# A hybrid decoder layer on one core: modulation sums, one feed-forward part and one x load put elsewhere

## The chip, the core and the metric

The kernel runs on one core of a Trainium2 chip. The core has a matrix engine (PE in the profile, with its weight loads as PEld), a vector engine (DVE), an activation engine (ACT), a general engine (POOL) and an engine that only issues transfers here (SP). Each engine works through its own instructions in order, and the engines wait for one another through semaphores. The metric is the time of one execution on the device in microseconds; lower is better. Shapes are partitions x elements.

## What is computed

One layer for a sequence of 1024 tokens of width 1024, in float32:

```python
mod = silu(cond) @ w_mod + b_mod            # nine vectors of 1024
sh1, sc1, g1, sh2, sc2, g2, sh3, sc3, g3 = split(mod, 9)

h = rms_norm(x) * (1 + sc1) + sh1
x = x + 0.5 * g1 * ((silu(h @ w_gate1) * (h @ w_up1)) @ w_down1)      # D_FF = 2816

h = rms_norm(x) * (1 + sc2) + sh2
b, c, v, u = split(h @ W_in, 4)                                       # 512 each
yA = b * causal_conv3(c * v)
yB = gelu(s5_scan(u) + D * u);  yB = yB * sigmoid(yB @ glu_w + glu_b)
x = x + g2 * (concat(rms_norm(yA), rms_norm(yB)) @ W_out)

h = rms_norm(x) * (1 + sc3) + sh3
x = x + 0.5 * g3 * ((silu(h @ w_gate2) * (h @ w_up2)) @ w_down2)
y = rms_norm(x)
```

## The kernel before

**Products.** Activations and weights are split into a high and a low half, and each product of a 128x128 weight with 128x512 activations is three matmuls (`mm3`, L333). The tokens are worked in two halves of 512 (h = 0, 1). The 2816 hidden columns of a feed-forward make 11 groups of 256.

**Seven products in place of eight.** In most groups the 2x2 block product of weights and activations is made by seven products of sums of blocks (`seven`, L575, gate first and then up). The sums of activations (A11, A12, A22, S1 to S4 in the code; tiles f, s and h3S in the profile) come from `combos` and `combos_last` (L543, L562) on DVE; the sums of weights (t1 to t4) are made on POOL by `combine` and `split_done` (L160, L168).

**Weights.** `stream` (L287) lists the weight arrays (1 MB each, tile raw) and the granules cut from them (tile w, two parts of 128x512, each with a high and a low half). `pump` (L182) makes the next granule when a ring slot is free: it loads the array if that isn't done, ACT copies the high half, and DVE subtracts to get the low half. Two raw tiles exist; a raw is reloaded when the granules before it have been cut. `take` hands granules to the products, `free` gives slots back.

**Which groups go where.** `LAST` (L39) names for each feed-forward the groups whose down projection is done plainly at its end. In the second feed-forward (names fb), group 0's four activation tiles stay in SBUF (`gu_evac`, L476) and its down projection (`down2`, L700: 96 matmuls and 16 DVE updates `x<-fb0d`) runs inside group 1, after the first of `seven`'s products. Groups 1 to 8 go to DRAM (`keep`, L482) and come back in `down7` (L655); groups 9 and 10 end it (the loop at the end of the kernel, tiles fb10d), where the last 256-token pieces of the final norm (n4, in the profile n_0 and n_256) follow.

**Modulation.** `mod_tile` (L466) makes a custom DVE instruction of 128x1024 (`wm<-wm,cact`, one eighth of a vector) and issues the fetch of a later array (512 KB, `wm<-in_wmod`). `side2` (L1132) makes them one at a time as a side task; `clock.period` says after how many clock ticks of the main work the next is put in. SC2, SH2 and G2 run from L1209 on, during the second half of the first feed-forward's down projection, into tiles of movA (a pool of 20). SC3, SH3 and G3 run from L1414 on, during the GLU and the output projection; for that the vector cact is written to DRAM at L849 and read back.

**The mixer.** `u` comes first (L1277 to L1292); as each of the four tiles ya0 to ya3 of u is done, `across` issues eight small transfers to u_d. The state space part goes in eight batches: `state_loads` (L1319) fetches ub, co and si; `states` (L1337) makes px on PE, copies it to X on ACT, swaps halves by transfers (swx), multiplies and scans on DVE, swaps again (swz) and adds to co on DVE; `outputs` (L1362) makes yy on PE, and then issues the fetches mk and mo for the next batch and ub, co, si for the one after that. The clock puts batch b's `states` and `outputs` among the matmuls of c and v (weights w103 to w110). cs is the tile in which c and v are multiplied. ub has two buffers; mi, mk and mo have one.

**Order.** The order on each engine is settled when the program is built, and differs from the order of the source lines. All transfers go through SP in order: one whose buffer is not free holds those behind it. They rotate over eight semaphores, so each waits for the one eight before it.

**x.** `load_x` (L327) brings x back in two parts after the side work; its second part (four transfers of 512 KB) is issued in `down7("fad0")` behind the product A12 of its first half (L1207).

Of the kernel before, what the change touches and what calls it, by code (L numbers as in the profile page):

```python
# [17 lines left out]
ALU = mybir.AluOpType  # L18
# [20 lines left out]
LAST = ((0, NGRP - 2, NGRP - 1), (NGRP - 2, NGRP - 1))  # L39
# [77 lines left out]
class Weights:  # L117
# [7 lines left out]

    def __init__(self, engines, srcs, granules, raw_bufs):
        self.V, self.A, self.SP, self.G = engines
        self.srcs, self.granules, self.raw_bufs = srcs, granules, raw_bufs
        self.left = [0] * len(srcs)
        self.combined = {j for pair in granules for j, c in pair if isinstance(c, str)}  # L130
        for pair in granules:
            for j, _ in pair:
                self.left[j] += 1
        self.raws, self.tiles, self.sums, self.kinds = [], [], {}, []
        self.given = self.freed = 0
        self.sums_pool = None
        self.slots = deque()
# [22 lines left out]
    def combine(self, j):  # L160

        f = self.sums_pool.tile([P, HALF], F32, tag="sums", name=f"sums{j}")[:]
        r = [self.raws[j][:, c * HALF : (c + 1) * HALF] for c in range(4)]
        self.G.tensor_tensor(out=f, in0=r[2], in1=r[1], op=ALU.subtract)  # L164
        self.G.tensor_tensor(out=r[1], in0=r[1], in1=r[0], op=ALU.subtract)  # L165
        self.sums[j] = {"t1": r[1], "t2": r[0], "t3": f, "t4": r[0]}

    def split_done(self, j, c):  # L168

        if j in self.combined and c in (0, "t2"):  # L170
            s, r = self.sums[j], self.raws[j][:, :HALF]
            if c == 0:
                self.G.tensor_tensor(out=r, in0=s["t3"], in1=r, op=ALU.add)  # L173
            else:
                self.G.tensor_tensor(out=r, in0=self.chunk(j, 3), in1=r, op=ALU.subtract)  # L175
# [56 lines left out]
def hymba_layer(ctx: ExitStack, tc, x_d, wm1_d, wmod_d, gu1_d, gs1_d, ds1_d, wl1_d, win_d, wout_d, glu_d, gu2_d, gs2_d, wd2_d, ds2_d, wl2_d, cols_d, cond_d, lam_d, bc_d, out_d):  # L232
# [54 lines left out]
    def stream(gu, gs, wd, ds, wl, m):  # L287


        for g in range(m):  # L290
            plain([gu[2 * g], gu[2 * g + 1]])
        for g in range(m, NGRP):
            j = len(srcs)
            inner = g == 1
            srcs.extend([gs[g - m, 0], wd, gs[g - m, 1]] if inner else [gs[g - m, 0], gs[g - m, 1]])
            seven = [(i, c) for i in (j, j + 1 + inner) for c in Weights.SEVEN]
            seven = [seven[i : i + 2] for i in range(0, 14, 2)]
            if inner:
                granules.extend(seven[:1] + [[(j + 1, 2 * q), (j + 1, 2 * q + 1)] for q in range(2)] + seven[1:])
            else:  # L300
                granules.extend(seven)
# [5 lines left out]
        plain([wl[i] for i in range(wl.shape[0])])  # L307

    stream(gu1_d, gs1_d, None, ds1_d, wl1_d, SEVEN_FROM[0])
    plain([win_d[i] for i in range(8)] + [glu_d] + [wout_d[i] for i in range(4)])  # L310
    stream(gu2_d, gs2_d, wd2_d, ds2_d, wl2_d, SEVEN_FROM[1])
    ws = Weights((V, A, SP, nc.gpsimd), srcs, granules, 2)
    ws.raw_pool = lambda i: rawp
# [162 lines left out]
    def gu_evac(fi, h, pg, pu, a_tiles, name):  # L476
        sg, af = t2k(f"{name}sg"), t2k(f"{name}af")
        A.activation(sg[:], pg[:], AF.Silu)
        V.tensor_tensor(out=af[:], in0=sg[:], in1=pu[:], op=ALU.mult)
        a_tiles[fi, h] = split_act(af[:], name + "a")  # L480

# [37 lines left out]

    def down(h, wd, groups, n, name, after):  # L520

        for d0 in range(0, KT, 4):
            outs = [ps(f"{name}d{d}_{h}") for d in range(d0, d0 + 4)]
            for q, a_tiles in enumerate(groups):
                for fi in range(2):
                    for i, o in enumerate(outs):
                        mm3(o[:], wd[2 * q + d0 // 4], 4 * fi + i, a_tiles[fi, h], q == fi == 0, q == len(groups) - 1 and fi == 1)
            for i, o in enumerate(outs):
                d = d0 + i
                V.scalar_tensor_tensor(out=x[d][h], in0=o[:], scalar=gate[:, n, d : d + 1], in1=x[d][h], op0=ALU.mult, op1=ALU.add)  # L530
                if after is not None:
                    after(d, h)
# [42 lines left out]
    def seven(name, between, place=1, kept=None, then=None):  # L575
# [4 lines left out]
        for side in "gu":  # L580
# [17 lines left out]
            for n, (left, b) in enumerate(SEVEN):  # L598
# [45 lines left out]
                if side == "g" and n == place:  # L644
                    between()
                if side == "u" and then is not None:
                    then(left)
        return a_tiles

# [50 lines left out]
    def down2(a_tiles, n, name, halves=(1, 0)):  # L700
        wd = ws.take(2)
        for dh in range(2):
            for h in halves:
                for i in range(4):
                    d = 4 * dh + i
                    o = ps(f"{name}d{d}_{h}")
                    for fi in range(2):
                        mm3(o[:], wd[dh], 4 * fi + i, a_tiles[fi, h], fi == 0, fi == 1)
                    V.scalar_tensor_tensor(out=x[d][h], in0=o[:], scalar=gate[:, n, d : d + 1], in1=x[d][h], op0=ALU.mult, op1=ALU.add)
            ws.free()  # L710

# [9 lines left out]
    es1 = ExitStack()  # L721
    cap = es1.enter_context(tc.tile_pool(name="cap", bufs=1))
# [126 lines left out]
    cact_d = scratch.tile([P, 1024], F32, name="cact_d")  # L849
    SP.dma_start(cact_d[:], cact[:])  # L850
# [345 lines left out]
    for g in range(SEVEN_FROM[0], NGRP):  # L1196
# [9 lines left out]
        seven(f"fa{g}", lambda: None, kept=kept[g], then=(lambda left: fetch_chunk(0, left)) if g == NGRP - 1 else None)  # L1206
# [71 lines left out]
    for h in range(2):  # L1278
# [8 lines left out]
        else:  # L1287
            ready(act2, h, KT)
            for i in range(4):
# [103 lines left out]

    wb = ws.take(4)
# [14 lines left out]
    mods_open = ExitStack()  # L1409
    wmp = mods_open.enter_context(tc.tile_pool(name="wmp2", bufs=1, side="right"))  # L1410
# [51 lines left out]
    clock.period = 1000  # L1462
# [11 lines left out]
    clock.period = 3  # L1474
# [8 lines left out]
    while clock.side:  # L1483
        clock.step()
    clock.period = 4
    mods_open.close()
    es2.close()
    movs["B"] = ctx.enter_context(tc.tile_pool(name="movB", bufs=12))
# [11 lines left out]
    ctx.callback(sums_open.close)  # L1500
    ctx.callback(first_open.close)

    def group0():

        a_tiles, pg, pu = {}, {}, {}
# [3 lines left out]
        gu_evac(0, 0, pg[0, 0], pu[0, 0], a_tiles, "fb0_0_0")  # L1509
# [5 lines left out]
        gu_evac(0, 1, pg[0, 1], pu[0, 1], a_tiles, "fb0_0_1")  # L1515
# [4 lines left out]
        for h in range(2):  # L1520
            gu_evac(1, h, pg[1, h], proj(u1, act3[h], f"fb0u1_{h}"), a_tiles, f"fb0_1_{h}")
        ws.free()
        return a_tiles

    clock.side.extend([combos(act3, "h3", "BAA"), combos_last(act3, "h3", "A")])
    a_prev = group0()
    kept = {g: kept_for(g, g not in LAST[1]) for g in range(1, NGRP - 1)}
    HOMES = dict(A11="B", S2="A", A12="B", S3="A", S1="B", A22="A", S4="A")
    lefts = [{left: [] for left in HOMES} for _ in range(CHUNKS)]
    a_last = {}  # L1530

    def fetch_last(left):
        if left == "A11":
            for h in range(2):
                for fi in range(2):
                    a_last[fi, h] = fetch(kept[NGRP - 2], f"A{h + 1}{fi + 1}", "B", f"fb{NGRP - 2}l")

    seven("fb1", lambda: down2(a_prev, 2, "fb0", (0, 1)), 0, kept[1])
    for g in range(2, NGRP - 1):
        seven(f"fb{g}", lambda: None, kept=kept[g])  # L1540
    a_prev = seven("fb10", lambda: None, then=lambda left: fetch_chunk(0, left, "fb"))
    down7("fbd0", lefts[0], 2, lambda left: fetch_chunk(1, left, "fb"))
    down7("fbd1", lefts[1], 2, fetch_last)
    n4 = {}
# [22 lines left out]

    for dh in range(2):
        wd = ws.take(2)
        for h in range(2):  # L1570
            for tok in PIECES[h] if dh else WHOLE:
                for i in range(4):
                    d = 4 * dh + i
                    o = ps(f"fb10d{d}_{h}_{tok.start}")
                    for q, (w, a) in enumerate(zip(wd, (a_last, a_prev))):
                        for fi in range(2):
                            mm3(o[:, tok], w, 4 * fi + i, a[fi, h], q == fi == 0, q == fi == 1, tok)
                    xs = x[d][h][:, tok]
                    V.scalar_tensor_tensor(out=xs, in0=o[:, tok], scalar=gate[:, 2, d : d + 1], in1=xs, op0=ALU.mult, op1=ALU.add)
                    for piece in PIECES[h] if not dh else [tok]:  # L1580
                        after2(d, h, piece)
        ws.free(2)
# [15 lines left out]
def _arrays(i):  # L1598
# [5 lines left out]
    for n in (1, 2):  # L1604
# [5 lines left out]
        if n == 2:  # L1610
            a["wd2"] = b[0].transpose(1, 2, 0, 3).reshape(P, 2, 1024)
# [31 lines left out]
_ORDER = ["x", "wm1", "wmod", "gu1", "gs1", "ds1", "wl1", "win", "wout", "glu", "gu2", "gs2", "wd2", "ds2", "wl2", "cols", "cond", "lam", "bc"]  # L1643
# [17 lines left out]
```

## Time and profile before

| | |
|---|---|
| runs, us | 1749.49 median of 3 (1746.47 to 1751.61) |
| profiled execution, its own time, us | 1752.1 |
| its span, first to last instruction, us | 1750.3 |
| mean granted PE clock | 0.989 |
| ACT, busy us (share) | 566.0 (32%) |
| POOL, busy us (share) | 351.1 (20%) |
| transfers, MB | 304.54 |
| share of the span on the chain that ended last | PE 76%, DVE 14%, DMA 5% |

The page gives each engine's busy time. A view of waits lists, for an engine, what it stood waiting for: us in total, how many times, and the longest. A view of windows gives each engine's busy time and instruction count in a stretch, with the TensorE clock granted in it, the share of time the transfer engines were busy and the rate in GB/s. In a timeline row stand the start, the duration, engine and line, the operation, output<-input, shape and how many instructions were joined; in brackets, the idle time before and what ended it. All instructions carry L107, the helper that records them, so tiles tell them apart.

### The profile page before, as it was taken

How to read it: one execution, taken by the hardware profiler on the slowest of the kernel's cores; microseconds unless marked ns; L12 is line 12 of the kernel's file. 1: busy time of each engine (PE TensorE's matmuls, PEld its weight loads, DVE VectorE, ACT ScalarE, POOL GpSimd, SP SyncE). 2: the span in 40 equal slices, each digit the busy share in tenths (PEclk: the TensorE clock that was granted, in tenths of full speed). 3: DMA queues.
4: the chain of work that ended last, by engine and by line, in shares of the span. 5: the costliest groups of instructions: out<-in, count | busy, mean ns of one | idle time of the engine just before them, and what ended most of it. 6: DMA issues, size and time to landing. Idle time of an engine off the chain costs nothing.

```text
span 1750.3 us, 20808 instructions
## 1 busy us (share of the span) xinstructions
PE 1677.9 (96%) x7532; PEld 1379.6 (79%) x7532; DVE 1300.6 (74%) x2286; ACT 566.0 (32%) x934; POOL 351.1 (20%) x241
## 2 busy tenths in 40 slices
PE   4999999999999999999999899989999999999996
PEld 3788887878787888887877778778888888888886
DVE  7999999999855687744656977967777666676656
ACT  4223234444322221332113424423343443322221
POOL 0000132222222221100000022023323322333211
PEclk9999999999999999999999999999999999999998
DMA  8245544444597877134654450113444334669312
GB/s 319 85 145 196 207 167 165 182 169 178 196 391 266 326 256 292 56 84 149 210 157 140 144 191 25 48 46 135 157 162 173 147 133 156 239 242 366 115 49 96
DMA packets 101080, 304.54 MB, mean 174 GB/s; under 512 B 19057, under 2 KB 34673, under 8 KB 89842
## 3 DMA queue, kind: packets, MB, share of 16 engines
q1 hardware_dynamic: 100978, 303.22, 48.4%
q8 instruction: 59, 0.97, 0.2%
q14 instruction: 43, 0.35, 0.1%
HBM read 212.47 MB, written 86.51 MB: 171 GB/s over the span
## 4 chain that ended last, share of the span: by engine, by line
PE 76%; DVE 14%; DMA 5%; issue 2%; POOL 1%; ACT 1%; SPq 1%; DVEq 0%; POOLq 0%; ACTq 0%
PE wo L107 4%; PE fald L107 3%; DVE w L107 3%; PE p L107 2%; PE fb10d L107 2%; PE fbd_0B L107 2%; PE fbd_1B L107 2%; PE u L107 2%; DMA swz<-si 2%; PE b L107 1%; DVE x L107 1%; PE c L107 1%; PE fa3u L107 1%; PE fb0g L107 1%; PE fa2g L107 1%
## 5 line engine op out<-in xcount | busy, mean ns | idle before, releaser
L107 ACT CAST w<-raw 128x512 fp32r<-128x512 f32 (+1 forms) x358 | 236.2, 689 | 484.3 <-issue 75.0
L107 DVE TENSOR_TENSOR w<-raw,w 128x512 fp32r<-128x512 f32 (+1 forms) x358 | 295.9, 845 | 107.3 <-ACT w L107 106.5
L164 POOL TENSOR_TENSOR sums<-raw 128x512 f32<-128x512 f32 x50 | 71.4, 1429 | 451.5 <-DMA raw<-in_gs 263.3
L173 POOL TENSOR_TENSOR raw<-sums,raw 128x512 f32<-128x512 f32 x50 | 77.7, 1554 | 371.1 <-DVE w L107 358.9
L175 POOL TENSOR_TENSOR raw<-raw 128x512 f32<-128x512 f32 x50 | 77.5, 1549 | 89.6 <-DVE w L107 73.0
L107 DVE CUSTOM_DVE_ANT_0 wm<-wm,cact 128x1024 f32<-128x1024 f32 x56 | 76.6, 1375 | 16.9 <-DMA wm<-in_wmod 16.9
L165 POOL TENSOR_TENSOR raw<-raw 128x512 f32<-128x512 f32 x50 | 77.3, 1547 | 3.2
L366 POOL TENSOR_TENSOR n3aq<-n3aq,n3aq 128x512 f32<-128x512 f32 x5 | 8.3, 1666 | 281.4 <-DMA wm<-in_wmod 255.7
L107 PE MATMUL p<-h,w 128*128 128x512 f32 x192 | 50.0, 423 | 8.0 <-DVE h L107 5.1
L107 DVE TENSOR_TENSOR w<-sums,w 128x512 fp32r<-128x512 f32 x50 | 52.5, 1063 | 3.6 <-ACT w L107 3.0
L107 PEld LDWEIGHTS p<-h,w 128*128 128x128 f32 x192 | 39.4, 207 | 18.4 <-DVE h L107 6.4
L107 PE MATMUL v<-h,w 128*128 128x512 f32 x192 | 46.9, 395 | 0.0
L107 PE MATMUL c<-h,w 128*128 128x512 f32 x192 | 46.6, 395 | 0.0
L107 PE MATMUL wo<-oa,w 128*128 128x512 f32 x192 | 45.6, 392 | 0.9 <-DVE w L107 0.7
L107 PE MATMUL b<-h,w 128*128 128x512 f32 x192 | 45.6, 394 | 0.0
L107 PE MATMUL wo<-ob,w 128*128 128x512 f32 x192 | 45.5, 392 | 0.0
L107 PE MATMUL u<-h,w 128*128 128x512 f32 x192 | 44.7, 392 | 0.2 <-DVE h L107 0.2
L107 PEld LDWEIGHTS wo<-oa,w 128*128 128x128 f32 x192 | 35.8, 188 | 9.0 <-DVE w L107 1.1
L107 PEld LDWEIGHTS u<-h,w 128*128 128x128 f32 x192 | 35.7, 188 | 8.2 <-DVE h L107 0.6
L107 PEld LDWEIGHTS wo<-ob,w 128*128 128x128 f32 x192 | 35.8, 188 | 7.7 <-DVE ob L107 0.4
L107 PEld LDWEIGHTS b<-h,w 128*128 128x128 f32 x192 | 35.6, 188 | 7.1
L107 PEld LDWEIGHTS c<-h,w 128*128 128x128 f32 x192 | 35.4, 188 | 7.0
(1565 smaller groups left out, 4056.2 us busy)
## 6 DMA issues: line engine op xcount, KB each, us to landing
raw<-in_gs SPq DMA_DIRECT2D x34, 1024.0 KB, 5.5
wm<-in_wmod SPq DMA_DIRECT2D x56, 512.0 KB, 5.3
raw<-in_ds SPq DMA_DIRECT2D x16, 1024.0 KB, 7.2
raw<-in_gu SPq DMA_DIRECT2D x10, 1024.0 KB, 7.0
mw<-in_wm SPq DMA_DIRECT2D x8, 1024.0 KB, 12.8
x<-in_x SPq DMA_DIRECT2D x16, 512.0 KB, 8.0
raw<-in_win SPq DMA_DIRECT2D x8, 1024.0 KB, 5.4
raw<-in_wl SPq DMA_DIRECT2D x5, 1024.0 KB, 6.7
```

Source lines behind the costliest of these rows:

```text
L107: r = getattr(self.engine, name)(*args, **kw)
L164: self.G.tensor_tensor(out=f, in0=r[2], in1=r[1], op=ALU.subtract)
L165: self.G.tensor_tensor(out=r[1], in0=r[1], in1=r[0], op=ALU.subtract)
L173: self.G.tensor_tensor(out=r, in0=s["t3"], in1=r, op=ALU.add)
L175: self.G.tensor_tensor(out=r, in0=self.chunk(j, 3), in1=r, op=ALU.subtract)
L366: nc.gpsimd.tensor_tensor(out=a, in0=a, in1=sq[:, :n], op=ALU.add)
```

## The change

It has four parts. Where the text below names A to D, it means these.

- **A.** Group 0 of the second feed-forward is kept in DRAM too, and its down projection is done with groups 9 and 10: three weights instead of two for each output, a third ring slot (ring1c), and for the first four outputs of the second half all four at a time.
- **B.** Group 1 of the second feed-forward has a function of its own (`seven_early`): A11, A12, A22 come before S1 to S4, and gate and up go side by side. Each granule takes one part from each of the two raw tiles, so that both raws are held until the group's last granule, w135.
- **C.** G2, SC3, SH3 and G3 (32 sums and 32 fetches) run in the second half of u and in the c and v stage, at period 3; cact stays in SBUF.
- **D.** The second part of the x load is issued behind the product A22 in place of A12.

```diff
-LAST = ((0, NGRP - 2, NGRP - 1), (NGRP - 2, NGRP - 1))
+LAST = ((0, NGRP - 2, NGRP - 1), (0, NGRP - 2, NGRP - 1))
...
+    EARLY = (0, 3, "t4", "t1", "t2", "t3", 2)
...
-        self.sums[j] = {"t1": r[1], "t2": r[0], "t3": f, "t4": r[0]}
+        self.sums[j] = {"t1": r[1], "t2": r[0], "t3": f, "t4": r[3 if j in self.early else 0]}
...
+        if j in self.early:
+            r0, r3 = (self.raws[j][:, q * HALF : (q + 1) * HALF] for q in (0, 3))
+            if c == 0:
+                self.G.tensor_tensor(out=r0, in0=self.sums[j]["t3"], in1=r0, op=ALU.add)
+            elif c == 3:
+                self.G.tensor_tensor(out=r3, in0=r3, in1=r0, op=ALU.subtract)
+            return
...
+            if g == 1:
+                two = j, j + 1
+                granules.extend([(j, c), (j + 1, c)] for c in Weights.EARLY)
...
+    EARLY = (("A11", "A"), ("A12", "A"), ("A22", "E"), ("S1", "C"), ("S2", "B"), ("S3", "D"), ("S4", "C"))
+
+    def seven_early(name, kept):
...
+        for left, b in EARLY:
+            (w,) = ws.take()
+            for q, side in enumerate("gu"):
+                bank, nm = banks[side], f"{name}{side}"
+                opens = b not in bank
+                if opens:
+                    bank[b] = ps(f"{nm}{b}")
+                for k in range(4):
+                    while len(blocks[left]) <= k:
+                        clock.step()
+                    mm3(bank[b][:], w, 4 * q + k, blocks[left][k], opens and k == 0, k == 3, more=not opens)
...
+                elif left == "S2":
+                    u2[side] = t2k(nm + "u2")
+                    add(u2, t1, side, "B")
+                elif left == "S3":
+                    u3[side] = t2k(nm + "u3")
+                    add(u3, u2, side, "D")
+                    add(t1, u3, side, "C")
...
+                elif left == "S4":
+                    add(u2, u2, side, "C")
...
+            ws.free()
...
-    cact_d = scratch.tile([P, 1024], F32, name="cact_d")
-    SP.dma_start(cact_d[:], cact[:])
...
-    down7("fad0", lefts[0], 0, lambda left: fetch_chunk(1, left), lambda left: load_x(range(2), (1, 3)) if left == "A12" else None)
+    down7("fad0", lefts[0], 0, lambda left: fetch_chunk(1, left), lambda left: load_x(range(2), (1, 3)) if left == "A22" else None)
     clock.period = 8
-    clock.side.append(side2(mod_mov, (SC2, SH2, G2)))
+    clock.side.append(side2(mod_mov, (SC2, SH2)))
...
             ready(act2, h, KT)
+            clock.period = 3
+            clock.side.append(side2(mod_mov, (G2, SC3, SH3, G3)))
...
+    while clock.side:
+        clock.step()
     wb = ws.take(4)
...
-    pools["cact"] = wmp.tile([P, 1024], F32, name="cact2")
-    SP.dma_start(pools["cact"][:], cact_d[:])
-    clock.period = 8
-    clock.side.append(side2(lambda name: wmp.tile([P, 1024], F32, tag="wm", name=name, bufs=2)[:], (SC3, SH3, G3)))
...
-        gu_evac(0, 0, pg[0, 0], pu[0, 0], a_tiles, "fb0_0_0")
+        gu_keep(0, 0, pg[0, 0], pu[0, 0], afs, kept, "fb0")
...
-    seven("fb1", lambda: down2(a_prev, 2, "fb0", (0, 1)), 0, kept[1])
+    seven_early("fb1", kept[1])
...
+    def last_part(dh, h, tok, tiles, free=False):
+        outs = {d: ps(f"fb10d{d}_{h}_{tok.start}") for d in tiles}
+        for q, (w, a) in enumerate(zip(wd, (*a_last, a_prev))):
+            for fi in range(2):
+                for d, o in outs.items():
+                    mm3(o[:, tok], w, 4 * fi + d % 4, a[fi, h], q == fi == 0, q == 2 and fi == 1, tok)
...
     for dh in range(2):
-        wd = ws.take(2)
+        wd = ws.take(3)
```

More of the change, by code (lines that the diff above doesn't have):

```diff
@@ L285, in plain, with stream @@
             srcs.append(a)
-    def stream(gu, gs, wd, ds, wl, m):
+    def stream(gu, gs, ds, wl, m):
+        two = ()
         for g in range(m):
@@ L518, in proj @@
         return o
[L520 to L532, printed above, removed]
     blocks = {}
@@ L573, in hymba_layer, with seven @@
     SECOND = (("A11", "A"), ("S2", "B"), ("A12", "A"), ("S3", "B"), ("S1", "C"), ("A22", "B"), ("S4", "C"))
-    def seven(name, between, place=1, kept=None, then=None):
+    def seven(name, kept=None, then=None):
         a_tiles, gate_, taken = {}, {}, []
@@ L643, in seven @@
                     ws.free()
-                if side == "g" and n == place:
-                    between()
                 if side == "u" and then is not None:
@@ L698, in down7 @@
                     (first, then)[p](left)
-    def down2(a_tiles, n, name, halves=(1, 0)):
-        wd = ws.take(2)
[L702 to L710, printed above, removed]
     def sums_opened():
@@ L1482, in hymba_layer @@
     w_out((4, 5, 6, 7), 0, 1)
-    while clock.side:
-        clock.step()
     clock.period = 4
-    mods_open.close()
     es2.close()
+    cap_open.close()
     movs["B"] = ctx.enter_context(tc.tile_pool(name="movB", bufs=12))
@@ L1499, in hymba_layer, with group0 @@
     sums_open, first_open = sums_opened()
[L1500 to L1505, printed above, removed]
+    def group0(kept):
+        afs, pg, pu = {}, {}, {}
         g0, u0, g1 = ws.take(3)
@@ L1566, in after2 @@
             ss.rstd(D, use, 6, 11)
+    def last_part(dh, h, tok, tiles, free=False):
[4 more added lines that the diff above has]
+                    mm3(o[:, tok], w, 4 * fi + d % 4, a[fi, h], q == fi == 0, q == 2 and fi == 1, tok)
+            if free:
+                ws.free()
+        for d, o in outs.items():
+            xs = x[d][h][:, tok]
+            V.scalar_tensor_tensor(out=xs, in0=o[:, tok], scalar=gate[:, 2, d : d + 1], in1=xs, op0=ALU.mult, op1=ALU.add)
+            for piece in PIECES[h] if not dh else [tok]:
+                after2(d, h, piece)
     for dh in range(2):
-        wd = ws.take(2)
+        wd = ws.take(3)
         for h in range(2):
             for tok in PIECES[h] if dh else WHOLE:
[L1572 to L1582, printed above, removed]
+                ds = range(4 * dh, 4 * dh + 4)
+                if h and not dh:
+                    last_part(dh, h, tok, ds, True)
+                else:
+                    for d in ds:
+                        last_part(dh, h, tok, [d])
+    ws.free(3)
     clock.drain()
```

91 lines of the change are left out of this document (56 added, 35 removed).

## The prediction

> **What bounds the kernel now.** I read the page first, then PE's waits, the granted clock in short windows, and timelines where the change acts.
>
> ```profile
> span 1750.3 us, 20808 instructions
> PE 1677.9 (96%) x7532; PEld 1379.6 (79%) x7532; DVE 1300.6 (74%) x2286; ACT 566.0 (32%) x934; POOL 351.1 (20%) x241
> ```
>
> PE is busy for 96% of the span. What can be won is the 72 us in which PE stands idle, and what it loses at a lower clock. PE's waits (us in total, times, longest) say where:
>
> ```profile
> PE yy L107 <- DVE co L107: 5.2, 6, 1.3
> PE fb0d L107 <- DVE x L107: 5.1, 4, 2.0
> ...
> PE nBabc L107 <- DVE nBarb L107: 3.9, 1, 3.9
> ...
> PE fad_0A L107 <- DVE w L107: 2.8, 2, 1.7
> ...
> PE n_0bc L107 <- DVE n_0rb L107: 2.5, 1, 2.5
> ...
> PE gl L107 <- DVE yg L107: 1.9, 1, 1.9
> PE fad_0B L107 <- ACT w L107: 1.8, 1, 1.8
> PE nAbbc L107 <- DVE nAbrb L107: 1.7, 1, 1.7
> ...
> PE px L107 <- DMA ub<-u_d: 0.6, 2, 0.3
> PE fald L107 <- DVE w L107: 0.5, 1, 0.5
> ```
>
> These are the places that the change touches: fad (first down projection), px and yy (mixer), gl, nA and nB (GLU and its norms), fb0d (group 0 of the second feed-forward), n_0 (end). Some waits cost a second time. These windows lie close behind waits of the list; after the busy times come granted clock, DMA share and GB/s:
>
> ```profile
> 547.00:550.40 3.40, 3.40 (x9) 2.67 (x8) 1.69 (x3) 2.18 (x4) 1.95 (x2) 0.50 0.77 283
> 557.20:560.60 3.40, 3.40 (x9) 2.62 (x9) 2.36 (x4) 1.33 (x3) 1.28 (x1) 0.50 0.00 0
> 953.20:956.60 3.40, 3.37 (x8) 2.70 (x9) 3.12 (x6) 0.00 (x0) 0.00 (x0) 0.51 0.00 0
> 983.90:987.30 3.40, 3.40 (x13) 3.01 (x13) 3.40 (x7) 1.89 (x4) 0.00 (x0) 0.50 0.62 176
> 1151.10:1154.50 3.40, 3.40 (x10) 2.37 (x9) 3.40 (x6) 0.46 (x1) 0.00 (x0) 0.50 0.02 5
> ```
>
> Each is 3.4 us at half clock and loses half of that, 1.7 us.
>
> **C, the mixer: the fetches in front of ub0.** DVE has room there and PE doesn't wait:
>
> ```profile
> 775.00:800.00 25.00, 25.00 (x113) 20.73 (x112) 4.29 (x4) 5.19 (x7) 0.00 (x0) 1.00 0.61 168
> ```
>
> So the 32 sums as such are covered. Their fetches aren't: they go into SP's queue between the u_d writes and the state-space fetches. In the changed program's order, ahead of the eight writes u_d<-ya3 and of ub0 now stand, among others, the fetches wm7_1_1 and wm7_2_0 and the load raw38. The sums take turns in four tiles, so wm7_1_1 waits for the sum of wm5_3_1, and on DVE that sum stands behind cs0<-v0_0, which needs the whole product v0_0. The rows of before for these instructions, DVE, PE and SP (start, us):
>
> ```profile
> 800.02 0.69 DVE L107 TENSOR_TENSOR cs<-cs,v 128x512 f32<-128x512 f32 x1 [2.65 <-PE v L107]
> ```
> ```profile
> 799.82 1.05 PE L107 MATMUL px<-ub,mi 128*128 128x128 f32 x8
> ```
> ```profile
> 786.92 5.83 SPq L107 DMA_DIRECT2D u_d<-ya  x8
> 792.79 0.91 SPq L107 DMA_DIRECT2D ub<-u_d  x2
> ```
>
> Here ub0 is issued at 792.8, well ahead of px0 at 799.8. That a fetch waits for a sum, and all behind it with it, already happens elsewhere, in the queue's own waits; and these are the durations (the sum from 650 to 1060, the last two landing times from 780 to 830):
>
> ```profile
> SPq L107 <- DVE scl L107: 67.9, 15, 17.8
> ```
> ```profile
> L107 DVE CUSTOM_DVE_ANT_0 wm<-wm,cact 128x1024 f32<-128x1024 f32 x36 | 51.7, 1447 | 15.8 <-DMA wm<-in_wmod 15.8
> ```
> ```profile
> raw<-in_win SPq DMA_DIRECT2D x2, 1024.0 KB, 6.0
> ```
> ```profile
> ub<-u_d SPq DMA_DIRECT2D x3, 256.0 KB, 3.4
> ```
>
> On the clock of before: cs0<-v0_0 ends at 800.7, the sum wm5_3_1 some 1.2 to 1.4 us later (802); then wm7_1_1 is issued. wm7_2_0 waits for one more sum (803.3), and raw38 follows. The eight u_d writes begin at 804 and take 5.8 in the row, because the last of them waits for the 1 MB load eight issues before it, as it will here with raw38. With 6.0 to 6.7 for that load ub0 is issued at about 810.8 and lands 3.4 later, at 814.1. On PE px0 stands right behind v0_0 and ahead of v0_1, so PE stands still from 799.8 to 814.1: +14.3. The lower bound leaves the raw load out: eight issues at 0.455 (two take 0.91) end at 807.6, ub0 lands at 811.0, +11.2. The upper gives the load 7.2 us and ub0 half as long again, 5.1, beside the fetches: +16.5. One half-clock window follows: +1.7.
>
> The rest of the mixer moves along. DVE has some 16 sums of 1.2 to 1.4 us (19 to 22 us) ahead of co0; PE has some 95 matmuls of 0.223 us (112 to 113 start in 25 us, the window row) ahead of its use in yy0, 21 us. They about meet, a wait between 0 and 3. The next one is surer: px2 stands only three matmuls (0.7 us) behind yy0, and its ub2 goes into the buffer that yy0 frees, behind mk1 and mo1 on SP. Three issues of 0.45 and a landing of 3.4 to 4.2 come to about 5.1, so +4.4 and a half window, +1.7; in before px2 came 5 us after yy0 and waited at most 0.3. For px4 to px7 I take 0.8 each, between 0.3 and 1.3 (the longest px and yy waits): +3.2. Before's yy and px waits, 5.8, fall away since PE comes later than co. Sum: 14.3 + 1.7 + 4.4 + 1.7 + 3.2 - 5.8 = +19.5. Bounds: 11.2 + 1.7 - 5.8 = +7 if the later waits don't come, and 16.5 + 1.7 + 5.9 + 1.7 + 5.2 - 5.8 = +25.
>
> **C, the GLU: waits that go.** On DVE, between nB's statistics and its result, stand three sums and a weight:
>
> ```profile
> L107 DVE CUSTOM_DVE_ANT_0 wm<-wm,cact 128x1024 f32<-128x1024 f32 x3 | 3.7, 1219 | 0.0
> L107 DVE TENSOR_TENSOR w<-raw,w 128x1024 fp32r<-128x1024 f32 x1 | 1.2, 1225 | 1.0 <-ACT w L107 1.0
> ```
>
> (DVE's groups from 975 to 984.) The sums alone are 3.7 of the 3.9 us that nBabc waits; the weight with its wait for ACT, 2.2, moves ahead as well. I take nBabc and nAbbc whole (3.9 + 1.7), 1.2 of gl's 1.9 (its yg comes late from DMA and ACT too), and the two half windows behind them (3.4): -10.2. Bounds: all of it -10.9; if only nBabc's wait goes and both half windows stay, about -3.
>
> **A and B, the start of the second feed-forward.** Group 0's 96 matmuls and 16 updates leave this stretch:
>
> ```profile
> L107 DVE SCALAR_TENSOR_TENSOR x<-fb0d,gate,x 128x512 f32<-128x512 f32 x16 | 11.5, 740 | 0.6 <-PE fb0d L107 0.6
> ```
> ```profile
> 1125.00:1150.00 25.00, 18.91 (x77) 13.66 (x76) 25.00 (x39) 6.48 (x11) 6.49 (x3) 1.00 0.12 42
> ```
> ```profile
> raw<-in_gs SPq DMA_DIRECT2D x2, 1024.0 KB, 4.8
> ```
> ```profile
> L173 POOL TENSOR_TENSOR raw<-sums,raw 128x512 f32<-128x512 f32 x50 | 77.7, 1554 | 371.1 <-DVE w L107 358.9 <-DVE dg L107 11.2
> ```
>
> Before's waits here go: 5.1 and the half window, -6.8. But DVE is full (25.00 of 25), its 52 instructions for the sums of activations stay, and 21 us of PE work that covered them go (96 x 0.223). From 1100 on DVE has 75 instructions up to w135; at 0.64 (39 in 25 us) and with 1.3 for ACT's copies they end at about 1149.5. PE reaches w131 about 0.7 late. S3 of the gate begins after 120 matmuls of group 1, 1121 + 26.8 + 0.7 = 1148.5, and needs the bank that fb1gu2 frees, behind w135: +2.0. The third new wait comes from the raws that B holds until w135. raw50 can be loaded only then and lands 4.8 later, at 1154.3; POOL's sum t1 takes two operations of 1.55 and ACT's copy 0.7, so w136 ends on DVE at about 1158.5. fb1gt1 stands behind it, and S4 of the gate, which PE reaches at 1156, writes the bank that fb1gt1 reads: +3.0. With one half window (+1.7) the new waits come to 7.4: net +0.6, from -6.8 (none of them) to +4 (two half windows, each wait longer by half). Group 0's four writes and four fetches of 512 KB meet a DMA share of 0.12 here; each is half of raw's 1 MB, so without that cover one costs at most its 4.8.
>
> **A, the end.** Six matmuls of 512 columns take 1.36 from start to start and of 256 columns 0.72:
>
> ```profile
> 1717.50 1.52 PE L107 MATMUL fb10d<-fb_0a,w 128*128 128x512 f32 x6
> 1718.86 0.88 PE L107 MATMUL fb10d<-fb9lA,w 128*128 128x256 f32 x6
> 1719.57 0.88 PE L107 MATMUL fb10d<-fb_1a,w 128*128 128x256 f32 x6
> ```
>
> 24 wide ones become 48 narrow: 48 x 0.12 - 24 x 0.227 = +0.3. More PE work now covers the pieces' statistics, but n_0's broadcast moves ahead of the last output and may make it wait: of n_0bc's 2.5 I take -1.2 (0 to -3).
>
> **D and C in the first feed-forward.** Only one x transfer changes sides with raw24 and raw25, which come some 1.3 us earlier (a 512 KB transfer less ahead of them, a quarter of raw's 4.8 or a little more): -1.3 of fad's waits and half windows (fad_0B 1.8, fad_0A 1.7, two windows 3.4), bounds 0 and -6.9. The 8 sums of G2 leave the end of that part, where fad_0A waits 1.1 (2.8 less 1.7) and fald 0.5: -1.5 (0 to -2).
>
> **Sum.** +19.5 - 10.2 + 0.6 + 0.3 - 1.2 - 1.3 - 1.5 = +6.2. The profiled execution's own time, 1752.1, becomes 1758.3. It lies 2.6 above the median of the runs shown; against that median, 1749.49, I forecast 1755.7 us.
>
> **A rule on the clock.** All half-clock windows above follow waits, and several of these are shorter than two microseconds (1.7, 1.8, 1.9). The Trainium skill, TensorE: Matmul & The Clock Gate, section What's actually happening, gives the lower clock for after at least one idle window of about 3.4 us. By that rule short waits would cost no clock, the GLU would give 3.4 less, and the sum would be +9.6, 1759.1. The rows show otherwise, and I go by them.
>
> **Rivals.**
> - Forecast, 1755.7: PE waits for ub0, then for ub2; the GLU's waits go. Chance 0.45, its own range 1750 to 1762.
> - Group 1's new order runs without waits. It decides whether raw50's first cut is through DVE before S3 of the gate ends on PE (about 1153). For it: DVE loses 11.5 us of updates. Against it: 25.00 of 25 busy, and the raws are held. Price -7.4: 1748.3, not slower. Chance 0.15.
> - The mixer catches up after ub0: DVE's chain and ub2 run in the shadow of the first stop, +7 in place of +19.5. For it: after it PE waits for nothing that isn't issued earlier. Against: yy0 itself frees ub2's buffer. 1743.2, faster. Chance 0.15.
> - The GLU's waits form again behind another releaser, since norms and splits stay chains on DVE: -3 in place of -10.2. Against it: the sums stand inside nB's chain. 1762.9. Chance 0.14.
> - Sums hold co on DVE in each batch, and yy waits each time: the mixer's +25, 1761.2. Against it: sums and matmuls of a batch about meet. Chance 0.11.
>
> **How the numbers follow.** 0.3% is 5.2 us, about what a measurement of this kernel tells from no change, so faster means below 1744.2, slower above 1754.7. The catching-up case gives half its chance to faster, and with group 1's gain most of it; all cases together: faster 0.18, same 0.27, slower 0.55. The range 1742 to 1767 runs from catching up with some of B's gain to the GLU's waits forming again with a long mixer; the likeliest case's own range is beside it above.
>
> **What would show it.** Right: px0 waits 11 to 16 us for ub0 and a half window follows; px2 waits about 4; nBabc and nAbbc are gone from the waits; fb1's S3 and S4 wait 2 and 3 us. Wrong: px0 without a wait (then the sums of C are free, and the time is below 1745); GLU waits in the list as before; no wait in fb1; or a long wait in a stage that isn't named here, such as b or the output projection, from fetches or sums that ran over.

## The result and the profile after

| | before | after |
|---|---|---|
| median, us (range of 3 runs) | 1749.49 (1746.47 to 1751.61) | 1773.16 (1768.78 to 1774.13) |
| profiled execution's own time, us | 1752.1 | 1774.13 |
| span, us | 1750.3 | 1772.4 |
| mean granted PE clock | 0.989 | 0.984 |

The changed kernel takes 1.0131 times as long, 95% interval 1.0095 to 1.0166: 23.7 us between the medians, where 6.2 were forecast. The direction was right; 1773.16 lies above the range of 1742 to 1767.

PE's waits in the kernel after (us in total, times, longest), the rows that answer to those of before:

```profile
PE px L107 <- DMA ub<-u_d: 26.8, 6, 16.6
...
PE fb1gA L107 <- ACT fb1gt L107: 4.1, 1, 4.1
...
PE px L107 <- issue: 3.2, 1, 3.2
...
PE yy L107 <- DVE co L107: 3.1, 3, 1.6
...
PE fb1gC L107 <- DVE fb1gt L107: 1.6, 1, 1.6
PE n_0bc L107 <- DVE n_0rb L107: 1.4, 1, 1.4
...
PE px L107 <- DMA y_d<-yg: 1.0, 1, 1.0
...
PE gl L107 <- DVE yg L107: 0.8, 2, 0.7
```

The waits for nBabc and nAbbc have left the list, gl's is 0.8. What fills it is px, the first product of each state-space batch: 31.0 us in its three rows where it was 0.6. (A row that ends in `issue` is a wait for which the view names no releaser.) To split the difference by stages, take where PE starts a product in each trace. Two rows of the view of a tile, before and then after (in each: duration min/median/max in ns, then the first and last start):

```profile
L107 PE MATMUL c<-h,w x192: 387/390/478, 783.5 to 878.7; 128*128 128x512 f32 x192
L107 PE MATMUL b<-h,w x192: 387/390/486, 894.0 to 945.8; 128*128 128x512 f32 x192
```
```profile
L107 PE MATMUL c<-h,w x192: 387/389/775, 782.0 to 912.7; 128*128 128x512 f32 x192
L107 PE MATMUL b<-h,w x192: 386/389/486, 929.5 to 981.0; 128*128 128x512 f32 x192
```

From the first c to the first b, which is the mixer, it is 110.5 us before and 147.5 after: +37.0. The same subtraction at other products gives the other stages:

| stage, from the first start of to that of | before, us | after, us | difference | forecast |
|---|---|---|---|---|
| start to c (first feed-forward, u) | 783.5 | 782.0 | -1.5 | -2.8 |
| c to b (mixer) | 110.5 | 147.5 | +37.0 | +19.5 |
| b to fb0g (GLU, norms, output projection) | 182.2 | 171.0 | -11.2 | -10.2 |
| fb0g to fb2gA, less the 21.4 us of matmuls that left | 93.6 | 91.7 | -1.9 | +0.6 |
| fb2gA to fb10d | 495.0 | 495.3 | +0.3 | 0 |
| fb10d to the end, with those 21.4 us added before | 85.5 | 84.9 | -0.6 | -0.9 |

All terms but one came within 3 us, and the differences add up to the 22.1 us between the two spans. The mixer alone holds the error.

Where the mixer loses: timeline of PE around px0 and px1, and of SP for the same time (start, duration, in brackets the idle time before and what ended it):

```profile
815.06 2.05 PE L107 MATMUL px<-ub,mi 128*128 128x128 f32 x8 [16.55 <-DMA ub<-u_d]
...
829.75 2.05 PE L107 MATMUL px<-ub,mi 128*128 128x128 f32 x8 [3.25 <-issue]
...
853.04 2.08 PE L107 MATMUL px<-ub,mi 128*128 128x128 f32 x8 [4.36 <-DMA ub<-u_d]
873.07 1.98 PE L107 MATMUL px<-ub,mi 128*128 128x128 f32 x8 [3.45 <-DMA ub<-u_d]
889.98 1.13 PE L107 MATMUL px<-ub,mi 128*128 128x128 f32 x8 [1.35 <-DMA ub<-u_d]
```
```profile
791.09 10.99 SPq L107 DMA_DIRECT2D wm<-in_wmod  x3
802.17 0.38 SPq L107 DMA_DIRECT2D raw<-in_win  x1
802.60 9.13 SPq L107 DMA_DIRECT2D u_d<-ya  x8
811.78 0.91 SPq L107 DMA_DIRECT2D ub<-u_d  x2
812.79 9.75 SPq L107 DMA_DIRECT2D wm<-in_wmod  x6
822.63 0.38 SPq L107 DMA_DIRECT2D mi<-mi_d  x1
823.11 1.17 SPq L107 DMA_DIRECT2D swx<-X  x2
```

The three fetches at 791.09 take 11 us to issue, since the second waits for a sum that stands on DVE behind cs0. Then come raw38, eight writes in 9.1 us, and ub0 at 811.78. That is the walk of the prediction, in its order. It is a little longer: ub0 is issued 13.3 us after v0_0 ends (at 798.51 here), where 11.0 were forecast, and raw38, put at 6.0 to 6.7 us, took 9.2 to land:

```profile
raw<-in_win SPq DMA_DIRECT2D x1, 1024.0 KB, 9.2
```

The next row of SP is what the prediction missed: six fetches stand between ub1 and mi1, and px1 needs mi1. Issued at 822.63, mi1 landed 7.0 us later, at 829.66, and px1 starts at 829.75. The same load in the kernel before, and its landing time there and here:

```profile
800.91 0.32 SPq L107 DMA_DIRECT2D mi<-mi_d  x1
```
```profile
mi<-mi_d SPq DMA_DIRECT2D x1, 256.0 KB, 2.7
```
```profile
mi<-mi_d SPq DMA_DIRECT2D x1, 256.0 KB, 7.0
```

So mi1 was late for two reasons. It was issued 5.5 us after px0's last product (817.11; before, within 0.1 us of it), and it took 4.3 us longer to land. As an estimate from these figures: PE waited 3.25 us of the 9.8, so some 6.5 us were covered, and neither reason alone would have made px1 wait. px2 and px3 wait for ub2 and ub3: ub3 was issued at 866.09, when a fetch eight issues before it had landed.

The granted clock of the stretch, in windows (busy times, then clock, DMA share, GB/s):

```profile
815.10:818.60 3.50, 3.50 (x12) 3.13 (x13) 0.08 (x1) 0.59 (x1) 0.00 (x0) 0.50 0.91 256
828.90:835.60 6.70, 5.85 (x18) 5.01 (x19) 6.41 (x11) 0.59 (x1) 0.00 (x0) 0.50 1.02 360
852.80:856.10 3.30, 3.06 (x11) 2.86 (x12) 3.27 (x8) 0.59 (x1) 0.00 (x0) 0.50 0.58 230
873.30:876.60 3.30, 3.30 (x13) 2.91 (x13) 3.30 (x9) 0.59 (x1) 0.00 (x0) 0.50 0.75 313
```

PE works 15.7 us of these at half clock and so loses 7.9 us, behind the first four px waits.

### The profile page after: what moved, and what is told of

The parts are those of the page before. It is cut to its first block, busy times and chain, and to the rows that moved or that the text cites. A ratio compares the mean times of both kernels' runs of the same rounds, so it can differ in the third digit from the quotient of the medians.

```text
span 1772.4 us, 20852 instructions
## 1 busy us (share of the span) xinstructions
PE 1679.9 (95%) x7556; PEld 1383.3 (78%) x7556; DVE 1285.6 (73%) x2270; ACT 565.5 (32%) x934; POOL 354.4 (20%) x241
## 4 chain that ended last, share of the span: by engine, by line
PE 67%; DVE 22%; DMA 5%; issue 4%; ACT 1%; SPq 1%; POOL 1%; DVEq 0%; ACTq 0%; POOLq 0%
PE wo L107 5%; DVE w L107 4%; PE fb10d L107 4%; PE fald L107 3%; PE c L107 2%; PE p L107 2%; PE u L107 2%; DVE f L107 2%; PE b L107 2%; PE fbd_1B L107 2%; PE fbd_0B L107 2%; PE fad_0B L107 1%; PE fad_1B L107 1%; PE v L107 1%; DMA ub<-u_d 1%
## 5 line engine op out<-in xcount | busy, mean ns | idle before, releaser
L167 POOL TENSOR_TENSOR sums<-raw 128x512 f32<-128x512 f32 x50 | 80.3, 1607 | 466.2 <-DMA raw<-in_gs 303.3
L185 POOL TENSOR_TENSOR raw<-raw 128x512 f32<-128x512 f32 x48 | 72.5, 1509 | 82.6 <-DVE w L107 65.7
L107 DVE CUSTOM_DVE_ANT_0 wm<-wm,cact 128x1024 f32<-128x1024 f32 x56 | 68.8, 1239 | 22.9 <-DMA wm<-in_wmod 22.9
L168 POOL TENSOR_TENSOR raw<-raw 128x512 f32<-128x512 f32 x50 | 77.5, 1549 | 3.4
L107 PE MATMUL px<-ub,mi 128*128 128x128 f32 x64 | 12.7, 360 | 31.0 <-DMA ub<-u_d 26.8
L107 PEld LDWEIGHTS v<-h,w 128*128 128x128 f32 x192 | 36.3, 195 | 7.2
```

The lines of the kernel that those rows point to most:

```text
L107: r = getattr(self.engine, name)(*args, **kw)
```

## The experiments

Three theories stood against one another. Q: a fetch that waits for its sum holds everything behind it on SP, so ub and mi come late. V: the 41 us of sums on DVE hold X, the scans and co. M: the 16 MB of fetches slow the state-space transfers by sharing the DMA engines with them. For each run the table gives the median, the ratio to runs of the kernel before on the same chip with its interval, the mixer stretch measured as above (110.5 before), and the stretch behind it, from the first b to fb0g (182.2 before), in which sums that run over show. The stretches are those of the one profiled execution of each run.

| run | median, us | ratio (95% interval) | mixer, us | over before | b to fb0g, us |
|---|---|---|---|---|---|
| changed kernel | 1773.16 | 1.0131 (1.0095 to 1.0166) | 147.5 | +37.0 | 171.0 |
| e1_without_C | 1747.78 | 0.9989 (0.9976 to 1.0001) | 109.6 | -0.9 | 183.2 |
| e2_C_alone | 1772.44 | 1.0130 (1.0112 to 1.0149) | 146.9 | +36.4 | 170.4 |
| e3_sums_no_fetch | 1742.40 | 0.9962 (0.9950 to 0.9974) | 117.0 | +6.5 | 171.0 |
| e4_fetch_small_read | 1755.83 | 1.0037 (1.0024 to 1.0050) | 131.5 | +21.0 | 170.8 |
| e5_pool_queue | 1762.98 | 1.0084 (1.0063 to 1.0105) | 138.6 | +28.1 | 171.1 |
| e6_start_behind_ub | 1758.49 | 1.0061 (1.0043 to 1.0079) | 131.9 | +21.4 | 169.9 |
| e8_A_without_B | 1772.58 (one run) | none | 146.0 | +35.5 | 170.3 |
| e9_period_6 | 1752.22 | 1.0024 (1.0013 to 1.0035) | 125.0 | +14.5 | 176.1 |
| e10_behind_ub_period_5 | 1747.65 | 0.9996 (0.9987 to 1.0006) | 117.2 | +6.7 | 177.0 |
| e11_G2_back_period_6 | 1744.44 | 0.9974 (0.9963 to 0.9985) | 115.0 | +4.5 | 173.1 |
| e12_G2_back_period_7 | 1741.97 | 0.9972 (0.9953 to 0.9991) | 112.7 | +2.2 | 172.9 |
| e13_before_with_e11_order | 1743.37 | 0.9961 (0.9948 to 0.9975) | 114.0 | +3.5 | 173.6 |

**C out, and C alone.** The first puts SC3, SH3 and G3 back behind the mixer and G2 into the first feed-forward, in the changed kernel; the second makes C's edits alone in the kernel before.

```diff
-            clock.period = 3
-            clock.side.append(side2(mod_mov, (G2, SC3, SH3, G3)))
...
+    clock.period = 8
+    clock.side.append(side2(lambda name: wmp.tile([P, 1024], F32, tag="wm", name=name, bufs=2)[:], (SC3, SH3, G3)))
```

> The changed kernel without part C (modulation sums back where they were before). By stages of the two traces C costs the mixer 36.7 us and gives 10.9 in the GLU; A, B and D together give about 4. If that split holds: 1773.2 - 36.7 + 10.9 = 1747 us, px waits under 1 us, gl/nA/nB waits back at about 7. If A, B or D also press on the mixer, px keeps waits of several us and the time stays above 1752.

> The kernel before with part C alone. Same split: 1749.5 + 36.7 - 10.9 = 1775 us, less about 1 for G2 leaving the first feed-forward; px waits near 30 us. If the loss needs A, B or D beside C, it is below 1765.

Measured 1747.78 and 1772.44. C explains the loss by itself, and the kernel with A, B and D alone can't be told from before (its interval holds 1).

**Sums without fetches.** Thirty of the 32 fetches are gone, all sums stay.

```diff
-            r = home(f"wm{n}_{b}_{i}")
-            SP.dma_start(r, wmod_d[n - 2, b, :, i, :])
+            if n not in (SC2, SH2) and "wm" in pools:
+                r = pools["wm"][i]
+            else:
...
```

> The changed kernel with all 32 sums in place, but 30 of the 32 fetches left out: the sums read two tiles that are fetched once, so gates and shifts come out wrong. Theory Q (fetches that wait for sums hold ub, mi and swx in SP's queue): px waits fall under 2 us, the mixer loses under 4 us against before, about 1738 us. Theory V (41 us of sums on DVE hold X, scans and co): the waits move from px to yy, 10 us or more, 1750 to 1770. Theory M (16 MB beside the state-space transfers): as Q here.

1742.40 against an expected 1738. V holds for a small part: px waits 0.6, but yy waits for co, once for long, and the mixer costs 6.5.

```profile
PE yy L107 <- DVE co L107: 8.6, 4, 7.0
PE px L107 <- DMA ub<-u_d: 0.6, 1, 0.6
```

**Fetches without sums.** All fetches stand at their places in SP's queue, but a tile is free as soon as POOL has read one column of it.

```diff
-        mod_vector(r, dst[:, d : d + 1])
+        if n in (G1, SC2, SH2):
+            mod_vector(r, dst[:, d : d + 1])
+        else:
+            nc.gpsimd.tensor_copy(dst[:, d : d + 1], r[:, 0:1])
```

> The changed kernel with all 32 fetches at their places in SP's queue, but each sum of these 32 replaced by a copy of one column on POOL, which is idle there; so a tile is free as soon as it has landed. Gates and shifts come out wrong. Theory Q: px0 waits under 3 us, mixer loses under 8 us, about 1742. Theory M: the bytes themselves cost: px0 still waits 10 us or more and the mixer loses over 25, above 1760. Theory V: as Q here, since DVE has no sums.

1755.83: between Q's 1742 and M's 1760. With no sum on DVE the fetches still cost 21.0 us in the mixer. px0's wait falls from 16.6 to at most 5.5, but the waits of the later batches stay:

```profile
PE px L107 <- DMA ub<-u_d: 16.9, 5, 5.5
PE px L107 <- issue: 1.4, 1, 1.4
```

Alone, the sums cost 6.5 and the fetches 21.0; the other 9.5 of the changed kernel's 37.0 come only with both. Q as first put is too narrow. But SP's queue isn't free in this run either: from 780 to 900 SP stands 19.6 us (15 times) until an earlier fetch has landed. So the 21.0 don't belong to the sharing of the DMA engines alone.

**The fetches on another queue.** POOL issues the 32 fetches.

```diff
-            SP.dma_start(r, wmod_d[n - 2, b, :, i, :])
+            (nc.gpsimd if n in (G2, SC3, SH3, G3) else SP).dma_start(r, wmod_d[n - 2, b, :, i, :])
```

> The changed kernel; the 32 fetches of part C are issued by POOL in place of SP, the sums stay on DVE. Theory Q (place in SP's queue): ub, mi and swx no longer stand behind fetches, px waits under 5 us, the mixer costs about 8 us (6 from the sums, as in the run without fetches), 1773 - 29 = 1745 us. Theory M (the bytes beside the state-space transfers): the 13 us by which the run with bare fetches lay above the run without fetches stay, 1755 to 1760, with landing times of ub, mi and swx still 6 us or more.

1762.98, which neither theory gave. The edit also changed the order on DVE: all sums came ahead of the first batch's `X<-co,X`, so this run can't separate the two. It shows both costs side by side in its waits and in the landing of the writes issued from 780 to 900 (KB each, median us to landing):

```profile
PE yy L107 <- DVE co L107: 18.1, 4, 16.7
PE px L107 <- DMA ub<-u_d: 9.5, 2, 9.4
```
```profile
u_d<-ya SPq DMA_DIRECT2D x17, 64.0 KB, 8.0
```

With no fetch ahead of them on SP, the small u_d writes still took 8.0 us to land; in the kernel before, 2.2 (median over the same stretch). ub0's issue then waits for one of them. mi1, issued right behind px0, took 6.2 to land in place of 2.7. So a place in SP's queue free of fetches doesn't restore the landing times while the fetches run beside.

**Start behind ub0 and ub1.** The edit moves the start of the sums behind the first two `state_loads`, at the same period.

```diff
-            clock.period = 3
-            clock.side.append(side2(mod_mov, (G2, SC3, SH3, G3)))
...
+    clock.period = 3
+    clock.side.append(side2(mod_mov, (G2, SC3, SH3, G3)))
     for b in range(NB):
         clock.after(20 + 16 * b, lambda b=b: states(b))
```

> The changed kernel; the 32 sums are started behind the fetches of the first two batches (the state_loads of 0 and 1), so that only three fetches stand ahead of ub0 and none that waits for a sum of this stage's DVE work. Theory Q: px0's 16.6 us and its half window go, while mi1 and ub2 still stand behind fetches (px1, px2, px3 wait 4 to 6 each as before or a little more): 1755 to 1760. If the first wait only moves on to px1 and px2, since the same 32 sums are now in a shorter stretch: 1765 or more.

1758.49, in Q's range. px0 runs without a wait, and the mixer falls from +37.0 to +21.4: ub0's place behind the waiting fetches is worth about 16 us. The later px waits stay.

```profile
PE px L107 <- DMA ub<-u_d: 15.1, 4, 5.9
```

**Spread.** The next two change the period alone, from 3 to 6 in the changed kernel and from 3 to 5 in the run just told.

```diff
-            clock.period = 3
+            clock.period = 6
             clock.side.append(side2(mod_mov, (G2, SC3, SH3, G3)))
```
```diff
-    clock.period = 3
+    clock.period = 5
     clock.side.append(side2(mod_mov, (G2, SC3, SH3, G3)))
     for b in range(NB):
```

> The changed kernel with the clock period of part C at 6 in place of 3, nothing else: the same 32 sums and fetches over about twice the stretch, with fewer fetches of 512 KB next to each other in SP's queue. If what costs is bursts and fetches that wait for sums behind cs0 (theory Q with bursts): px0 waits under 6, all px together under 15 us, 1752 to 1757. If the 16 MB beside the mixer's own transfers cost however they are spread (theory M): 1765 or more.

> The sums started behind the first two batches' fetches as in the run before, now at period 5 in place of 3. That run's px waits were 16 us in all, with mi, swx and mk landing 6 to 8 us after issue behind bursts of four or five fetches. Bursts: landing times of mi and swx fall to 3 to 5, px waits under 8, 1748 to 1752. Bytes however spread: 1757 or more. If sums run over into the b stage's start, PE waits show there.

1752.22 and 1747.65. The second makes a pair with the run just told: the same 32 fetches and the same start, only the spacing differs. The mixer falls from +21.4 to +6.7. Not all of that is won: with the wider spacing sums and fetches run on into the next stretch, and b to fb0g takes 177.0 in place of 169.9. Over both stretches the spacing wins 7.6 us. For each, the window 780 to 905 (PE, PEld, DVE, ACT, POOL, clock, DMA share, GB/s) and the issues from 780 to 905; period 3 first, then period 5:

```profile
780.00:905.00 125.00, 107.55 (x496) 89.04 (x495) 87.42 (x153) 20.68 (x29) 0.00 (x0) 0.92 0.84 267
```
```profile
wm<-in_wmod SPq DMA_DIRECT2D x29, 512.0 KB, 6.8
...
mi<-mi_d SPq DMA_DIRECT2D x6, 256.0 KB, 6.2
```
```profile
780.00:905.00 125.00, 117.41 (x577) 97.33 (x576) 89.16 (x153) 23.11 (x33) 0.00 (x0) 0.97 0.84 265
```
```profile
wm<-in_wmod SPq DMA_DIRECT2D x24, 512.0 KB, 6.0
...
mi<-mi_d SPq DMA_DIRECT2D x7, 256.0 KB, 4.3
```

The DMA engines are equally busy (0.84) and move the same GB/s, yet mi lands 2 us sooner and PE gains 10 us in the stretch. So the load of the DMA engines over the stretch doesn't set the price. That fetches issued in groups ahead of the small transfers do is the reading that is left, but the pair doesn't isolate it: 24 fetches fall into the window in place of 29.

**G2 back.** G2's 8 sums return to the first feed-forward; 24 remain behind ub1, at period 6 and then 7.

```diff
-    clock.side.append(side2(mod_mov, (SC2, SH2)))
+    clock.side.append(side2(mod_mov, (SC2, SH2, G2)))
...
-    clock.period = 5
-    clock.side.append(side2(mod_mov, (G2, SC3, SH3, G3)))
+    clock.period = 6
+    clock.side.append(side2(mod_mov, (SC3, SH3, G3)))
     for b in range(NB):
```

> As the one before with G2's 8 sums back in the first feed-forward, so 24 sums and 12 MB in the mixer, at period 6. Bursts: px waits under 5 us, the GLU still gives 10, the first feed-forward costs 1 to 1.5 again: 1744 to 1747, faster than both kernels. Bytes however spread: three quarters of the 20 us stay, 1755.

> As the run with G2 back and period 6, at period 7. If spreading further still helps the mixer, it costs under 3 us there (4.3 at period 6) and the time is 1741 to 1744; if what is left comes from the sums on DVE (6 us in the run without fetches), or sums run over into the b stage, 1744 to 1748.

1744.44 and 1741.97, some 0.3% faster than before (both intervals lie below 1); the intervals overlap, so period 7 isn't shown to be better. In the first of them px has nearly no wait, and what is left is yy's, as in the run without fetches:

```profile
PE yy L107 <- DVE co L107: 6.0, 4, 2.8
...
PE px L107 <- DMA ub<-u_d: 0.8, 1, 0.8
```

**That order alone.** The same placement at period 6, in the kernel before, without A, B and D.

```diff
+    clock.period = 6
+    clock.side.append(side2(mod_mov, (SC3, SH3, G3)))
     for b in range(NB):
...
-    clock.period = 8
-    clock.side.append(side2(lambda name: wmp.tile([P, 1024], F32, tag="wm", name=name, bufs=2)[:], (SC3, SH3, G3)))
```

> The kernel before with the modulation order of that run alone (SC3, SH3, G3 behind the first two batches' fetches, period 6; G2 in the first feed-forward), without A, B and D. By stages: mixer +4.3, GLU -8.9, so about -4 to -5: 1744 to 1745. A, B and D alone measured -1.9; if the two add up, the run with both (1744.4) should have been at 1743. If this one is not faster than before, the gain of that run came from A, B and D.

1743.37, ratio 0.9961 (0.9948 to 0.9975): the gain comes from the placement of the sums. A, B and D add nothing that could be measured on top of it. The mixer still costs 3.5 here, and b to fb0g gives 8.6.

**B undone.** Group 1 goes back to `seven`, A stays.

```diff
-    seven_early("fb1", kept[1])
+    seven("fb1", kept=kept[1])
```

> The changed kernel with group 1 in the order of the other groups (part B undone, A kept). S1 to S3 then come as second to fourth product, with 21 us of PE work less in front of them than before: if DVE's sums of activations bound this stretch, PE waits 10 us or more in fb1 and the time is 1780 or more; if not, fb1 waits under 6 us as in the changed kernel, about 1773.

1772.58 in a single run, which is the changed kernel's time. fb1 waits 6.0 us there (5.7 in the changed kernel), so DVE's sums of activations don't bind as I feared. From fb0g to fb2gA it takes 93.3 where the changed kernel takes 91.7, so B's order is worth 1.6 us in this pair of traces.

```profile
PE fb1gC L107 <- ACT h3S L107: 6.0, 2, 5.3
```

## Why the prediction was wrong, step by step

- **ub0 behind the fetches (+14.3 and a half window, 1.7).** Right in mechanism; in size 16.55 and 1.8, just over the upper bound of 16.5. v0_0 ended 1.3 us earlier than in the kernel before, so ub0's issue at 811.78 is 2.3 us later than the forecast 810.8, by raw38's longer landing. With the start behind ub1 px0 doesn't wait and the mixer is 15.6 us shorter, which shows the cause.
- **"The rest of the mixer moves along": the step that failed.** The walk followed ub0 and ub2, put px1 and px3 at nothing, and didn't ask which other transfers each px needs. mi has one buffer, so mi1 is fetched only when px0 has run, and by then six fetches of 512 KB stood ahead of it on SP: px1 waited 3.25 us for it. ub3 stood behind further fetches: px3 waited 3.45. Neither was in the sum: +6.7. The walk also took its landing times from the kernel before; beside the fetches raw38 took 9.2 us in place of 6.0 to 6.7, and mi1 7.0 in place of 2.7.
- **Clock.** I counted two half windows in the mixer (3.4); the four px waits brought four stretches that lose 7.9: +4.5.
- **px2 (+4.4).** 4.36. px4 to px7 (+3.2): 1.35 and 1.0 in rows, the others below 1, 3.4 in all.
- **yy and px waits of before (-5.8).** yy still waits 3.1: +3.1 against the forecast.
- **Together.** 31.0 of px, 7.9 of clock, 3.1 of yy, less 5.8: 36.2 of the 37.0. The upper bound of +25 came from stretching the waits that I had listed; it couldn't hold one that wasn't listed. That the transfers themselves would be slower went into the bounds for raw38, ub0 and ub2 alone.
- **GLU (-10.2).** -11.2 with the output projection. The three sums inside nB's chain were its waits: with them put back (e1_without_C) nBabc waits 3.9 us again and nAbbc 1.7.
- **Start of the second feed-forward (+0.6).** -1.9. The new waits came to 5.7 us and one half window, as forecast in sum (5.7 and 1.7), but not where forecast, so the agreement is luck: S3 doesn't wait, S4 waits 1.6, and the longest, 4.1, stands at A12, behind ACT's copy of the first product. That copy stands on ACT behind two weights for which POOL made the sums:

```profile
1152.28 0.62 ACT L107 CAST w<-raw 128x512 fp32r<-128x512 f32 x1 [4.56 <-POOL raw L178]
1153.95 0.62 ACT L107 CAST w<-raw 128x512 fp32r<-128x512 f32 x1 [1.05 <-POOL raw L178]
...
1154.97 0.58 ACT L107 COPY fb1gt<-fb1gA 128x512 f32<-128x512 f32 x1
```

  POOL's sums were not in that part of the prediction's walk. 1.0 of the 2.5 us between -1.9 and +0.6 are two shorter waits of fb0d in the kernel before that went too; for the rest the traces show no cause.
- **End (-0.9).** -0.6; n_0bc waits 1.4 in place of 2.5.
- **First feed-forward (-2.8).** Not confirmed. fald starts at 664.7 in place of 667.8, but 1.5 of that had been gained ahead of the down projection, and runs with the same first feed-forward (e6, e8, e10) start fald between 664.1 and 666.4. A half window at 746.9, which before didn't have, took 1.7 back. It stands behind a wait of 1.3 us; e6 has the same wait and no such window. A term of this size can't be read from one trace:

```profile
746.90:750.30 3.40, 3.40 (x9) 2.63 (x10) 2.40 (x13) 0.00 (x0) 0.00 (x0) 0.50 0.69 246
```

- **Rivals.** The one in which the sums hold co in each batch had the right stage and sign, but not the mechanism: yy's waits fell, px's grew. The Trainium skill's rule on the clock (TensorE: Matmul & The Clock Gate, What's actually happening: the lower clock after an idle window of about 3.4 us) agrees with the stretches behind px waits of 16.55, 4.36 and 3.45 us; px1's 3.25 lies a little under its figure, and it doesn't account for the windows behind waits of 1.7 to 1.9 us of before. The +9.6 that I gave for it was worked out wrongly: of the two half windows of the GLU one follows nBabc's wait of 3.9 us, and the window behind fb0d's waits, at most 2.0 us each, was left in.

What stays open: how the 21 us of the run with bare fetches divide between waiting in SP's queue and sharing the DMA engines. For px1 of the changed kernel the trace parts them, 5.5 us and 4.3; for the stage as a whole no run does. The run that should have, with POOL's queue, changed DVE's order as well; it shows only that the landing times stay long with no fetch in SP's queue.

## What to carry to other kernels

Before filling idle time of one engine with side work, list for the next few steps of the main chain every transfer that each needs, with its place in the issuing queue, and not only the first that comes late. A tile with one buffer, as mi here, can be fetched only when the step before has used it. Side fetches that share an in-order queue with a latency chain want to be started behind the chain's first loads and spaced out: here that turned 1.3% slower into no difference (ratio 0.9996), and with G2's sums back in the first feed-forward into 0.3 to 0.4% faster. Look at the next stretch too: what is spread too thinly runs over into it, as at period 5. When a bound is made by stretching listed waits, leave room for one that isn't on the list.

## What the runs showed of the hardware

Equal DMA share and rate can go with quite different landing times. At share 0.84 and 265 to 267 GB/s, mi's 256 KB landed in 6.2 or 4.3 us in the median depending on how the side fetches were spaced, against 2.8 in the kernel before, at share 0.60 and 180 GB/s.

DVE and POOL were slow beside each other, in turn. In the changed kernel's group 1 of the second feed-forward, DVE's additions of 128x512 take 0.68 us each, and 1.73 while POOL makes its sums. Just before, it is the other way about: one addition on POOL takes 9.47 us, where its others take 1.6 to 1.7, and DVE's beside it run at their 0.69. What decides which of them gives way the runs don't show. DVE's rows, then POOL's:

```profile
1139.42 0.69 DVE L107 TENSOR_TENSOR h3S<-f,h3S 128x512 fp32r<-128x512 f32 x1
...
1145.95 3.47 DVE L107 TENSOR_TENSOR f<-h 128x512 f32<-128x512 f32 x2
...
1154.39 0.68 DVE L107 TENSOR_TENSOR f<-h 128x512 f32<-128x512 f32 x1
```
```profile
1136.00 9.47 POOL L167 TENSOR_TENSOR sums<-raw 128x512 f32<-128x512 f32 x1 [23.32 <-DMA raw<-in_gs]
1145.55 1.63 POOL L168 TENSOR_TENSOR raw<-raw 128x512 f32<-128x512 f32 x1
1147.14 3.42 POOL L176 TENSOR_TENSOR raw<-sums,raw 128x512 f32<-128x512 f32 x2
```
